# The order of TensorE products that use 128 rows and 64 rows of the array, in two stages of a two-layer encoder

## The chip, the cores and the metric

The kernel runs on one core of a Trainium2 chip. It is one launch; the metric is the device time of that launch in microseconds (us). Three runs of the kernel before are shown below, and a profile of one execution.

Five engines run side by side, each through its own list of instructions in order, and wait for each other by semaphores: TensorE (PE, matrix products into PSUM; PEld is its loading of the stationary operand), VectorE (DVE), ScalarE (ACT), GpSimd (POOL) and SyncE (SP, which here issues DMAs).

## The reference, cut to what matters

Two layers on a sequence of 1024 tokens by 1024 channels, float32. Each layer: normalise, project by a wide matrix, a mixer, gate, project back, add.

```python
def _even_mixer(...):      # layer 0: four mLSTM heads and four DeltaNet heads, each forward and backward in time
    out_a = sigmoid(mo) * head_rms(mlstm(q, k, v) + flip(mlstm(flip(q), ...)))
    out_b = head_rms(gdn(q, k, v) + flip(gdn(flip(q), ...)))
def _mlstm_chunkwise(...): # per chunk, state cmat (64 x 128 per head) and nvec
    num = w_int * einsum('bhld,bhde->bhle', qc, cmat) + einsum('bhls,bhse->bhle', sc, vc)
    den = w_int * einsum('bhld,bhd->bhl', qc, nvec) + sum(sc, -1)
def _odd_mixer(...):       # layer 1: a convolution of 31 taps and dilated attention of eight heads of 64 channels
    sc = einsum('bhrnid,bhrnjd->bhrnij', qb, kb) * dh ** -0.5 + bias    # per group of a dilation
    p = exp(sc - max(sc)); o = p @ v / sum(p)
```

## The kernel before, in words

**Products.** All products go through the helper `mm` (L119) and all transposes through `tr` (L134), so the profile shows them as L120 and L135; they are told apart by the tiles' names. Wide projections (`prod`, names `z`, `mo`, `dv`, `aq`, `ak`, `av`, `gb`, `ga`, `y`) split each float32 operand in a high and a low part and make three products of 128 rows, 128 columns and 512 elements. A product whose operands stand on 128 partitions uses all 128 rows of the array; one on 64 partitions uses a 64-row tile of it, rows 0 to 63 or 64 to 127. A plain float32 product (the mLSTM's, and the transposes) is two instructions, or passes, in the trace; those on split parts are one.

**mLSTM (layer 0, `mlstm_step`, L776).** The sequence is cut in 8 chunks of 128 tokens, and step j handles chunk j forward and chunk 7-j backward (two "direction-steps"). For each, PSUM tiles `num` (two banks, one for the even heads e=0 and one for the odd, e=1; each holds two heads q=0, 1) collect two products per head: `qt` times the state `mC` (64 rows: a head has 64 key channels) and the weights `E` times the values `mv` (128 rows, 129 elements). VectorE then makes the denominators `den`, and the output is stored; `Cps` holds the products for the next state. From step 1 on each direction-step has four products of each kind. The products of the gates' projections (`z`, `mo`) and of DeltaNet's values (`dv`) are put among them by the scheduler.

**Attention (layer 1, `attention`, L1301).** Heads are handled in four pairs `p_`, each in 8 steps i of 128 queries, so 32 steps. For each of the pair's heads e, one PSUM bank `sc` takes four products: queries `aq` times the high part of the keys `ak` (128 rows, since the low part of the queries stands in the other 64 rows) and `aq` times the low part of the keys `akl` (64 rows: 0 to 63 for e=0, 64 to 127 for e=1), each for the near group (columns c0:c1, contiguous) and for the group of dilation 4 (columns 256:512, read with a step of four elements, `r4`). The kernel issues near high, near low, dilated high, dilated low, and then the next head. VectorE adds the bias to `sc` and finds the extremes (L1336, L1338: the result is `pt`), ScalarE takes the exponentials, TensorE transposes them (`pT`, four per head), VectorE copies these to `PT` (L1363), and TensorE multiplies them by the values into `ob` (column tiles of 64). ScalarE copies `ob` to `o2`, and a DMA writes it to `od_d`. `sc` has two banks (tag "A", `BANKS` L83), one for each head.

While a pair is worked on, projections stand between its steps: `z` for the first and the third pair, `aq`, `ak`, `av` of the next pair, and, in the last pair, the first products `y` of the output.

**What sets the order.** The order on each engine isn't written by hand: a list scheduler of the framework makes it from the order of the program, the tiles' dependences and its own estimate of what is ready. An engine executes its list strictly in that order. So a change in the program's order also moves instructions that it doesn't name.

Of the kernel before, what the change touches and what calls it, by code (L numbers as in the profile page):

```python
# [17 lines left out]
P = 128  # L18
T = 1024
D = 1024  # L20
# [10 lines left out]
def t5_bucket(rel):  # L31
    # the bucket of a relative position, as the reference has it (32 buckets, 1024 at most)
    n = np.abs(rel)
    large = 8 + (np.log(np.maximum(n, 1).astype(np.float32) / np.float32(8)) / np.float32(np.log(128.0)) * np.float32(8)).astype(np.int32)
    large = np.minimum(large, 15)
    return (rel > 0).astype(np.int32) * 16 + np.where(n < 8, n, large)


def consts():
    # tables that depend on shapes alone  # L40
# [16 lines left out]
def trunk(ctx, tc, x, c, norm_g, ada_w, ada_b, ev_w_in, ev_m_gate_b, ev_dn_dt_bias, ev_dn_a_log,  # L57
# [42 lines left out]
    def behind(ins, first):  # L100
        # ins is issued after first, without a wait
# [17 lines left out]
    def mm(o, l, r, s, e):  # L119
        return nc.tensor.matmul(o, lhsT=l, rhs=r, start=s, stop=e).ins  # L120
# [16 lines left out]
    # vectors by channel  # L137
# [41 lines left out]
    def ada_sum(tiles, name):  # L179
        # sum over the chunks of d of c's SiLU times the weights; the sum over partitions is left to TensorE  # L180
# [89 lines left out]
    # gate rows: 0.. i, 32.. f, 64.. beta, 96.. decay; in each, 4 forward heads then 4 backward ones  # L270
# [86 lines left out]
    # DeltaNet keys  # L357
# [13 lines left out]
    def conv5(xp, cidx, y):  # L371
        # twice the SiLU of the convolution
# [7 lines left out]
    def conv5s(xp, cidx, y):  # L380
        # the same with ScalarE and GpSimd
# [39 lines left out]
    def modulation():  # L421
        # the rest of the modulation, a few rows of the weights with every chunk of a projection
# [79 lines left out]
    # chunk totals (rows 32.. and 96..)  # L502
# [9 lines left out]
    # running maxima of a = i - b in each chunk  # L512
# [49 lines left out]
    # the same by token: [token, chunk, 8 * quantity + dir * 4 + head]  # L562
# [24 lines left out]
    def sel_mask(ap, d):  # L587
        # keep row position l >= s (forward) or l <= s (backward); partitions are s
# [30 lines left out]
    # the lanes' results and those transposed  # L619
# [5 lines left out]
    def dn_system(ch):  # L625
# [13 lines left out]
        # the backward direction's transposed: upper triangles too  # L639
# [7 lines left out]
    def dn_inverse(n):  # L647
        # in each lane the inverse of I minus a strictly triangular 64 x 64 block, in place;
        # lanes: direction, block, chunk, head; the backward direction's blocks are transposed
# [50 lines left out]
    # gates by channel: the norm's weight, the SiLU of z and for the mLSTM half the output gate  # L700
# [56 lines left out]
    def mlstm_weights(ch):  # L757
        # weights of the pairs in the chunk, for both directions
# [18 lines left out]
    def mlstm_step(j):  # L777
        for d in range(2):
# [12 lines left out]
            pss = [bank(nm("num"), (P, 2, P + 1), "BA"[d]) for e in range(2)]  # L791
            for q in range(2):
                for e in range(2):
                    h = 2 * q + e
                    hp = slice(e * 64, e * 64 + 64)
                    if j > 0:
                        mm(pss[e][:, q, :], qt[hp, q, :], mC[d][hp, q, :], True, False)
                    pace["cps"] = mm(pss[e][:, q, :], E[:, h, :], mv[ch // 2][:, ch % 2, h, :], j == 0, True)
# [41 lines left out]
    def m_k(j):  # L840
        in0(256 + j * P, "mk", lambda hf, ps: nc.scalar.mul(out=mk[j][:, half(hf)], in_=ps, mul=0.125))
        # by token, times the weights that they enter the state with
# [44 lines left out]
    # DeltaNet over the chunks  # L887
# [4 lines left out]
    def dn_step(j):  # L892
        for d in range(2):
# [4 lines left out]
            # (I + N)^-1, transposed  # L898
# [16 lines left out]
            # decays  # L915
            # weights of the pairs in the chunk: for both directions at the first visit
# [15 lines left out]
            # v'  # L932
# [15 lines left out]
            # state  # L948
# [21 lines left out]
            # output  # L970
# [15 lines left out]
    def load_wout(w, gate, tags="h" * 16):  # L986
        # the output weights, each column times its gate
# [22 lines left out]
    def out_tile(parts, wo, use):  # L1010
        # parts [channel, token] by chunk -> psum [token, D]
# [10 lines left out]
    # scales of the summed DeltaNet outputs  # L1022
# [79 lines left out]
    # the last two by halves of the tokens: the first half's pages are free early  # L1102
# [25 lines left out]
    # the negated relative bias by relative position, one row per head  # L1128
# [13 lines left out]
    # each row again at a pitch one longer than the pitch it is read with: Toeplitz tiles  # L1142
# [46 lines left out]
    def taps(cidx):  # L1189
        # the middle one first: it reaches every token  # L1190
        for j in [15] + [j for j in range(31) if j != 15]:
            yield j - 15, cw1[:, j * 4 + cidx:j * 4 + cidx + 1]

    def conv31s(cidx, xp):
        # the same with ScalarE and GpSimd
# [65 lines left out]
    def qkv(p_):  # L1261
        # q and k as float32r parts. For each head q has its high part in the head's own rows and its low part
        # in the other rows, k has its high part in both
# [45 lines left out]
    def attention(p_, t_in):  # L1309
# [6 lines left out]
        for i in range(8):  # L1316
# [3 lines left out]
            # by group: both heads' sums, denominators and negated maxima  # L1320
            o2 = wk.tile([P, 2, 132], F32, tag="o2", name=nm("o2"))
            for e in range(2):
                hp = slice(64 * e, 64 * e + 64)
                ps = bank(nm("sc"), tag="A")
                q1, k1 = slice(i * P, i * P + P), slice(i * P - 64 + c0, i * P - 64 + c1)
                q2 = slice(hb * P, hb * P + P)
                mm(ps[:, c0:c1], Q[e][:, q1], K[e][:, k1], True, False)
                mm(ps[:, c0:c1], Q[e][hp, q1], KL[hp, k1], False, True)
                mm(ps[:, 256:512], r4(Q[e])[:, i // 2, q2], r4(K[e])[:, i // 2, :], True, False)
# [244 lines left out]
```

## Time and profile before

| | |
|---|---|
| runs | 1588.95, 1594.66, 1594.58 us; median 1594.58 |
| span of the profiled execution, first to last instruction | 1592.5 us |
| busy PE / PEld / DVE / ACT / POOL | 88% / 69% / 61% / 40% / 38% of the span |
| mean granted TensorE clock | 0.916 |
| mLSTM products `num` | 381 to 590 us of the span |
| attention scores `sc` | 1052 to 1497 us of the span |

The profile has a span and no separate time for the execution; its span lies between the runs and 2.1 us under their median. Busy shares are averages over stages with different limits, so each stage is read by itself. The granted clock is 1 at 2.4 GHz and 0.5 at 1.2 GHz. A product's record lasts longer than the time until the next one begins, because products are pipelined: what one costs the engine is the distance from its start to the next one's start.

### The profile page before, as it was taken

The page shows a single profiled execution, that of the slowest core. Times are in us where ns is not written, and L with a number is a line of the kernel's source. Part 1 is how long each engine was busy: PE and PEld are TensorE (multiplying, and loading weights), DVE is VectorE, ACT ScalarE, POOL GpSimd, SP SyncE. Part 2 cuts the span into 40 slices and gives each one's busy share as a digit, 9 for nine tenths or more (in the row PEclk, how much of TensorE's full clock was granted, in tenths as well). Part 3 has the DMA queues.
Part 4 walks back from the last instruction along what each step waited for, and adds up shares of the span by engine and source line. Part 5 has one row for each costly group of instructions (what it writes and reads, how often), then busy time and mean ns, then how long its engine had stood idle before and what let it go on. Part 6 is the DMA issues. An engine that isn't in the chain of part 4 may idle for free.

```text
span 1592.5 us, 20530 instructions
## 1 busy us (share of the span) xinstructions
PE 1407.7 (88%) x7195; PEld 1091.6 (69%) x7195; DVE 978.0 (61%) x1712; ACT 636.1 (40%) x1481; POOL 599.3 (38%) x433
## 2 busy tenths in 40 slices
PE   3978758878788999889999988689999999999998
PEld 2767646656566777778778666567776777776786
DVE  6799256999796531447745449998664433334444
ACT  5355266332444423444543233344226433324322
POOL 3452525653463521212341159986042123022210
PEclk9999878999879999889999989888899989996899
DMA  9323589345646867565552721001141142142432
GB/s 319 87 79 83 124 177 229 93 143 149 161 143 220 271 210 156 152 154 169 189 187 78 155 66 40 27 27 47 41 139 41 58 152 85 52 145 76 154 103 106
DMA packets 235659, 202.50 MB, mean 127 GB/s; under 512 B 38592, under 2 KB 198868, under 8 KB 235428
## 3 DMA queue, kind: packets, MB, share of 16 engines
q1 hardware_dynamic: 214755, 190.70, 42.1%
q10 hardware_dynamic: 20800, 10.49, 2.3%
q8 instruction: 57, 0.93, 0.2%
q14 instruction: 47, 0.38, 0.1%
HBM read 146.87 MB, written 57.93 MB: 129 GB/s over the span
## 4 chain that ended last, share of the span: by engine, by line
PE 40%; DVE 9%; DMA 4%; ACT 2%; issue 1%; POOL 0%; SPq 0%; POOLq 0%; ACTq 0%; DVEq 0%
PE y L120 9%; PE z L120 8%; DVE u L1216 7%; PE sc L120 6%; PE av L120 3%; PE ob L120 2%; PE pT L135 2%; PE aq L120 2%; PE ak L120 2%; DMA z_d<-nb_d 1%; ACT junk L1036 1%; PE gb L120 1%; PE vps L135 1%; PE T L120 1%; DMA E<-gc_d 0%
## 5 line engine op out<-in xcount | busy, mean ns | idle before, releaser
L240 POOL TENSOR_TENSOR wlo<-wraw,whi 128x1024 fp32r<-128x1024 f32 x60 | 157.2, 2621 | 239.6 <-ACT whi L239 228.2
L1216 DVE SCALAR_TENSOR_TENSOR u<-xp,cw,u 128x1009 f32<-128x1009 f32 (+14 forms) x90 | 172.8, 1920 | 2.1
L1206 POOL TENSOR_TENSOR u<-u,cv 128x512 f32<-128x512 f32 (+15 forms) x60 | 119.0, 1986 | 23.1 <-ACT cv L1205 19.8
L431 POOL TENSOR_TENSOR macc<-macc,ada 128x512 f32<-128x512 f32 x56 | 86.7, 1548 | 72.7 <-ACT ada L429 60.7
L120 PE MATMUL z<-hhi,whi 128*128 128x512 f32 x256 | 110.0, 430 | 2.3 <-DVE zt L709 2.3
L120 PE MATMUL z<-hlo,whi 128*128 128x512 f32 x256 | 109.5, 428 | 0.0
L120 PE MATMUL z<-hhi,wlo 128*128 128x512 f32 x256 | 108.4, 424 | 0.0
L239 ACT CAST whi<-wraw 128x1024 fp32r<-128x1024 f32 x60 | 62.5, 1042 | 95.2 <-PE gb L120 16.3
L120 PE MATMUL y<-wohi,mhi 128*128 128x512 f32 x240 | 96.9, 405 | 1.2 <-ACT mhi L1006 1.2
L120 PE MATMUL y<-wolo,mhi 128*128 128x512 f32 x240 | 96.1, 401 | 0.0
L120 PE MATMUL y<-wohi,mlo 128*128 128x512 f32 x240 | 95.4, 399 | 0.6 <-DVE mlo L1007 0.5
L665 DVE TENSOR_TENSOR NL<-NL,iv 128x440 f32<-128x440 f32 (+40 forms) x106 | 91.7, 894 | 0.5
L662 DVE TENSOR_TENSOR iv<-NL 128x440 f32<-128x440 f32 (+40 forms) x106 | 86.2, 845 | 1.6 <-DMA ada<-in_ada_w_dram 0.2
L1363 DVE COPY PT<-pT 128x512 f32<-128x512 f32 x48 | 32.6, 689 | 78.1 <-PE pT L135 78.0
L590 POOL TENSOR_SCALAR_AFFINE_SELECT E<-E 128x512 f32<-128x512 f32 x32 | 22.9, 715 | 147.1 <-DMA E<-nmu_d 55.3
L429 ACT ACTIVATE ada<-ada,cs 128x512 f32<-128x512 f32 x56 | 40.3, 724 | 80.6 <-DMA ada<-in_ada_w_dram 80.6
L120 PE MATMUL sc<-ak,aq 128*128 128x256 f32 (+1 forms) x128 | 61.7, 482 | 5.1 <-DVE o L1338 3.2
L120 PE MATMUL sc<-akl,aq 64*128 64x256 f32 (+1 forms) x128 | 63.6, 497 | 0.0
L120 PEld LDWEIGHTS z<-hhi,whi 128*128 128x128 f32 x256 | 52.1, 203 | 16.3 <-DVE zt L709 3.0
L1205 ACT ACTIVATE cv<-xp,cw 128x512 f32<-128x512 f32 (+15 forms) x60 | 42.2, 717 | 52.7 <-POOL u L1206 52.5
L120 PEld LDWEIGHTS z<-hlo,whi 128*128 128x128 f32 x256 | 51.9, 203 | 12.6 <-issue 1.6
L120 PEld LDWEIGHTS z<-hhi,wlo 128*128 128x128 f32 x256 | 52.0, 203 | 11.8 <-issue 0.6
(448 smaller groups left out, 3748.8 us busy)
## 6 DMA issues: line engine op xcount, KB each, us to landing
wraw<-in_ev_w_in_dram SPq DMA_DIRECT2D x32, 512.0 KB
ada<-in_ada_w_dram SPq DMA_DIRECT2D x64, 256.0 KB
wraw<-in_od_w_in_dram ACTq DMA_DIRECT2D x20, 512.0 KB
x<-in_x_dram SPq DMA_DIRECT2D x16, 512.0 KB
ada<-in_ada_w_dram SPq DMA_DIRECT2D x16, 512.0 KB
od_d<-o SPq DMA_DIRECT2D x64, 66.0 KB
n<-od_d SPq DMA_DIRECT2D x4, 1056.0 KB
E<-nmu_d SPq DMA_DIRECT2D x16, 256.0 KB
```

The source lines that it names most:

```text
L120: return nc.tensor.matmul(o, lhsT=l, rhs=r, start=s, stop=e).ins
L135: nc.tensor.transpose(o, i, ident[:k, :k])
L239: nc.scalar.copy(out=hi, in_=raw)
L240: nc.gpsimd.tensor_tensor(out=lo, in0=raw, in1=f(hi), op=ALU.subtract)
L429: nc.scalar.mul(out=t_ if k else acc, in_=t_, mul=cs[:, k:k + 1])
L431: nc.gpsimd.tensor_tensor(out=acc, in0=acc, in1=t_, op=ALU.add)
L662: nc.vector.tensor_tensor(out=t_, in0=NL[:, a_:b_, k:k + 1].to_broadcast([P, b_ - a_, m]), in1=NL[:, k:k + 1, k + 1:64].to_broadcast([P, b ...
L665: nc.vector.tensor_tensor(out=NL[:, a_:b_, k + 1:64], in0=NL[:, a_:b_, k + 1:64], in1=t_, op=ALU.add)
L1205: nc.scalar.mul(out=t_, in_=xp[:, lo + d:hi + d], mul=w_)
L1206: nc.gpsimd.tensor_tensor(out=y[:, lo:hi], in0=y[:, lo:hi], in1=t_, op=ALU.add)
L1216: nc.vector.scalar_tensor_tensor(out=y[:, lo:hi], in0=xp[:, lo + d:hi + d], scalar=w_, in1=y[:, lo:hi], op0=ALU.mult, op1=ALU.add)
L1363: nc.vector.tensor_copy(out=PT, in_=tb)
```

## The change: what it does

`mlstm_step`: the four `E`-by-`mv` products (128 rows) of a direction-step come first, one after the other, and then the four `qt`-by-`mC` products (64 rows) in the order q=1, q=0, the heads e=0 and e=1 in turn. `attention`: both heads' banks are taken together; the four 128-row products of both heads come first, then the four 64-row products. Only the first product into a bank starts an accumulation, and the last ends it, since the groups in one bank now overlap in time. The products themselves, their number and their operands stay. Comments were taken out of the file as well, and `mm` has a new argument with which the groups of one bank may overlap.

```diff
-    def mm(o, l, r, s, e):
-        return nc.tensor.matmul(o, lhsT=l, rhs=r, start=s, stop=e).ins
+    def mm(o, l, r, s, e, shared=False):
+
+        return nc.tensor.matmul(o, lhsT=l, rhs=r, start=s, stop=e, skip_group_check=shared).ins
...
             for q in range(2):
                 for e in range(2):
-                    h = 2 * q + e
-                    hp = slice(e * 64, e * 64 + 64)
-                    if j > 0:
-                        mm(pss[e][:, q, :], qt[hp, q, :], mC[d][hp, q, :], True, False)
-                    pace["cps"] = mm(pss[e][:, q, :], E[:, h, :], mv[ch // 2][:, ch % 2, h, :], j == 0, True)
+                    pace["cps"] = mm(pss[e][:, q, :], E[:, 2 * q + e, :], mv[ch // 2][:, ch % 2, 2 * q + e, :],
+                                     q == 0 or j == 0, j == 0, q > 0 and j > 0)
+            if j > 0:
+                for q in (1, 0):
+                    for e in range(2):
+                        hp = slice(e * 64, e * 64 + 64)
+                        pace["cps"] = mm(pss[e][:, q, :], qt[hp, q, :], mC[d][hp, q, :], False, q == 0, q > 0)
...
+            q1, k1 = slice(i * P, i * P + P), slice(i * P - 64 + c0, i * P - 64 + c1)
+            q2 = slice(hb * P, hb * P + P)
+            pss = [bank(nm("sc"), tag="A") for e in range(2)]
+            for e in range(2):
+                mm(pss[e][:, c0:c1], Q[e][:, q1], K[e][:, k1], True, False)
+                mm(pss[e][:, 256:512], r4(Q[e])[:, i // 2, q2], r4(K[e])[:, i // 2, :], False, False, True)
             for e in range(2):
                 hp = slice(64 * e, 64 * e + 64)
-                ps = bank(nm("sc"), tag="A")
-                q1, k1 = slice(i * P, i * P + P), slice(i * P - 64 + c0, i * P - 64 + c1)
-                q2 = slice(hb * P, hb * P + P)
-                mm(ps[:, c0:c1], Q[e][:, q1], K[e][:, k1], True, False)
-                mm(ps[:, c0:c1], Q[e][hp, q1], KL[hp, k1], False, True)
-                mm(ps[:, 256:512], r4(Q[e])[:, i // 2, q2], r4(K[e])[:, i // 2, :], True, False)
-                mm(ps[:, 256:512], r4(Q[e])[hp, i // 2, q2], r4(KL)[hp, i // 2, :], False, True)
+                mm(pss[e][:, 256:512], r4(Q[e])[hp, i // 2, q2], r4(KL)[hp, i // 2, :], False, False, True)
+                mm(pss[e][:, c0:c1], Q[e][hp, q1], KL[hp, k1], False, True)
+            for e in range(2):
+                hp = slice(64 * e, 64 * e + 64)
+                ps = pss[e]
```

TensorE's order before, one direction-step of the mLSTM (step 5; `qt` products have 64 rows, `E` products 128; the numbers tell the tiles apart, `num_3185` is the bank of the even heads and `num_3186` that of the odd):

```order
L120 MATMUL num_3185<-mC_2856,qt_3179 128x129
L120 MATMUL num_3185<-mv_1456,E_3177 128x129
L120 MATMUL num_3186<-mC_2856,qt_3179 128x129
L120 MATMUL num_3186<-mv_1456,E_3177 128x129
L120 MATMUL num_3185<-mC_2856,qt_3179 128x129
L120 MATMUL num_3185<-mv_1456,E_3177 128x129
L120 MATMUL num_3186<-mC_2856,qt_3179 128x129
L120 MATMUL num_3186<-mv_1456,E_3177 128x129
```

The same direction-step now:

```order
L121 MATMUL num_3185<-mv_1456,E_3177 128x129
L121 MATMUL num_3186<-mv_1456,E_3177 128x129
L121 MATMUL num_3185<-mv_1456,E_3177 128x129
L121 MATMUL num_3186<-mv_1456,E_3177 128x129
L121 MATMUL num_3185<-mC_2856,qt_3179 128x129
L121 MATMUL num_3186<-mC_2856,qt_3179 128x129
L121 MATMUL num_3185<-mC_2856,qt_3179 128x129
L121 MATMUL num_3186<-mC_2856,qt_3179 128x129
```

Seven changes between 64 and 128 rows inside the block have become one. Of the 56 `qt` products of the program, 54 stood alone between 128-row products before; now 12 blocks have four and one has eight.

TensorE's order before, one step of the first pair's attention (step 4; `ak` products have 128 rows, `akl` 64; `sc_8529` is e=0, `sc_8554` e=1):

```order
L135 MATMUL pT_8485<-ident,pt_8479 128x128 x4
L120 MATMUL sc_8529<-ak_8044,aq_8042 128x256
L120 MATMUL sc_8529<-akl_8046,aq_8042 128x256
L120 MATMUL sc_8529<-ak_8044,aq_8042 128x256
L120 MATMUL sc_8529<-akl_8046,aq_8042 128x256
L135 MATMUL pT_8510<-ident,pt_8504 128x128 x2
L120 MATMUL sc_8554<-ak_8045,aq_8043 128x256
L120 MATMUL sc_8554<-akl_8046,aq_8043 128x256
L120 MATMUL sc_8554<-ak_8045,aq_8043 128x256
L120 MATMUL sc_8554<-akl_8046,aq_8043 128x256
L120 MATMUL z_1433_8822<-hlo_1122_6871,whi_8817 128x512
```

The same step now (e=0 is `sc_8529`, e=1 is `sc_8530`), and behind it step 1 of the same pair:

```order
L136 MATMUL pT_8490<-ident,pt_8484 128x128 x4
L136 MATMUL pT_8510<-ident,pt_8504 128x128 x4
L121 MATMUL sc_8529<-ak_8044,aq_8042 128x256 x2
L121 MATMUL sc_8530<-ak_8045,aq_8043 128x256 x2
L121 MATMUL sc_8529<-akl_8046,aq_8042 128x256 x2
L121 MATMUL sc_8530<-akl_8046,aq_8043 128x256 x2
L121 MATMUL z_1433_8822<-hhi_1117_6866,wlo_8818 128x512
```

```order
L121 MATMUL sc_8364<-ak_8044,aq_8042 128x256
L136 MATMUL pT_8321<-ident,pt_8315 128x128 x2
L121 MATMUL sc_8364<-ak_8044,aq_8042 128x256
L121 MATMUL sc_8364<-akl_8046,aq_8042 128x256 x2
L121 MATMUL sc_8365<-ak_8045,aq_8043 128x256 x2
L121 MATMUL sc_8365<-akl_8046,aq_8043 128x256 x2
```

In the one step the order is that of the program; in the other the scheduler kept the heads apart and grouped within each head. Before, each of the 128 `akl` products stood alone; now 37 blocks have two, 8 have four, 5 have three, and 7 stand alone. In 18 of the 32 steps some product of e=1 now stands ahead of the last product of e=0; before that was so in 4 steps.

## Rows read from the trace of the kernel before

**Rows 1.** Chain of waits that ended last: shares of the span by line.
```profile
by line: PE y L120 9.3%; PE z L120 7.7%; DVE u L1216 6.6%; PE sc L120 6.1%; PE av L120 2.7%; PE ob L120 2.4%; PE pT L135 2.4%; PE aq L120 2.1%; PE ak L120 1.6%; issue 1.5%; DMA z_d<-nb_d 1.3%; ACT junk L1036 0.8%; PE gb L120 0.7%; PE vps L1
...
679.78 4.62 DMA at_d<-E
...
1452.92 2.28 DMA od_d<-o
```
**Rows 2.** Stretches: us, busy PE, PEld, DVE, ACT, POOL (instructions), clock, DMA share, GB/s.
```profile
440.00:600.00 160.00, 147.57 (x699) 108.11 (x699) 98.97 (x231) 64.53 (x137) 68.19 (x64) 0.93 0.67 212
600.00:780.00 180.00, 163.67 (x1116) 142.34 (x1115) 92.03 (x233) 76.57 (x209) 33.06 (x39) 0.92 0.63 171
...
1063.00:1200.00 137.00, 135.21 (x722) 101.10 (x723) 97.64 (x159) 48.14 (x116) 59.65 (x33) 0.89 0.22 68
1200.00:1317.00 117.00, 113.78 (x659) 85.07 (x658) 50.86 (x125) 57.43 (x129) 28.62 (x14) 0.93 0.28 92
1317.00:1426.00 109.00, 108.72 (x658) 81.64 (x657) 39.61 (x123) 35.34 (x99) 24.46 (x12) 0.97 0.24 76
1426.00:1502.00 76.00, 73.24 (x432) 52.00 (x433) 34.95 (x95) 33.00 (x90) 18.54 (x8) 0.78 0.44 138
```
**Rows 3.** Waits 592 to 780 us: who for whom, us, times, longest.
```profile
ACT E L615 <- POOL E L590: 52.8, 15, 9.4
POOL E L590 <- DMA E<-gc_d: 43.9, 10, 11.2
```
**Rows 4.** TensorE's timeline around attention: start, us, operation, rows*columns, shape, count.
```profile
1102.62 1.09 PE L135 MATMUL pT<-ident,pt 128*128 128x128 f32 x8
1103.47 0.36 PE L120 MATMUL sc<-ak,aq 128*128 128x256 f32 x1
1103.76 0.38 PE L120 MATMUL sc<-akl,aq 64*128 64x256 f32 x1
1104.07 0.60 PE L120 MATMUL sc<-ak,aq 128*128 128x256 f32 x1
1104.60 0.59 PE L120 MATMUL sc<-akl,aq 64*128 64x256 f32 x1
1105.12 0.38 PE L120 MATMUL sc<-ak,aq 128*128 128x256 f32 x1
...
1106.80 0.50 PE L120 MATMUL z<-hhi,wlo 128*128 128x512 f32 x1
```
**Rows 5.** TensorE's timeline in the mLSTM, three places.
```profile
448.44 0.68 PE L120 MATMUL num<-mv,E 128*128 128x129 f32 x4 [1.27 <-issue]
448.88 0.47 PE L120 MATMUL z<-hhi,wlo 128*128 128x512 f32 x1
...
490.05 0.72 PE L120 MATMUL S<-mq,mk 64*128 64x128 f32 x8
490.70 0.50 PE L120 MATMUL mo<-hhi,wlo 128*128 128x512 f32 x1
...
498.87 0.49 PE L120 MATMUL num<-mC,qt 64*128 64x129 f32 x2 [0.34 <-DVE E L772]
499.28 0.49 PE L120 MATMUL num<-mv,E 128*128 128x129 f32 x2
...
505.13 0.49 PE L120 MATMUL num<-mv,E 128*128 128x129 f32 x2
```
**Rows 6.** Tile sc: its products (ns min/median/max) and the first bias add.
```profile
L120 PE MATMUL sc<-akl,aq x128: 351/586/600, 1052.5 to 1497.2; 64*128 64x256 f32 x112, 64*128 64x192 f32 x16
...
L1338 DVE CUSTOM_DVE_ANT_0 pt<-sc,bias x64: 409/419/422, 1066.8 to 1499.7; 128x256 f32<-128x256 f32 x64
```
**Rows 7.** Waits 1060 to 1500 us: who for whom, us, times, longest.
```profile
DVE pt L1336 <- DMA od_d<-o: 16.4, 12, 4.1
...
PE sc L120 <- DVE o L1338: 3.2, 3, 1.5
```

## The prediction

> **What bounds the kernel now.** I read the busy table by stretch first, then the chain of waits, then TensorE's timeline inside the two stages that the change touches, and last the waits around them. In the attention stage TensorE is the bound: over the four stretches from 1063 to 1502 us it is busy 135.2 + 113.8 + 108.7 + 73.2 = 431 of 439 us [rows 2], and VectorE, the next, 223. The chain of waits says the same from the other side: the score products `sc` alone hold 6.1% of the span on it, 97 us [rows 1]. These are nearly all of them: the reader is to see that 32 steps of some 3.3 us (1103.47 to 1106.80 [rows 4]) make 107 us, less what is put between them. Whatever a step's scores cost less, the end comes earlier, as long as TensorE stays the bound.
>
> The mLSTM stage is less clear. TensorE is busy 147.6 of 160 us from 440 to 600 [rows 2], but the chain, followed back from the end, stops at 679.78 us at a DMA [rows 1] and says nothing of earlier work. Behind it, from 600 to 780 us, TensorE is busy 163.7 of 180 us, while ScalarE waits 52.8 us for GpSimd's masks and GpSimd 43.9 us for DMAs [rows 2, 3]: a stage that is part TensorE, part a sequence of other engines.
>
> **The price of a change between 64 and 128 rows.** In the mLSTM, pairs of passes of `qt` and `E` products alternate: from 498.87 to 505.13 us are 15 pairs, 0.417 us each [rows 5]. Four passes of `E` products that follow each other take 448.44 to 448.88, 0.11 us each [rows 5], so a pair without a change is 0.22. A change costs 0.417 - 0.22 = 0.197 us. The scores fit: eight transposing passes of 128 columns, with no change, take 1102.62 to 1103.47, 0.106 each; a near score product between two changes takes 1103.47 to 1103.76 and 1103.76 to 1104.07, 0.30; that is one change and 0.10 [rows 4]. A dilated one takes 0.53 (1104.07, 1104.60, 1105.12 [rows 4]), one change and 0.33.
>
> What a change costs must be partly the load of the stationary operand, which without a change goes beside the product ahead, and partly the time in which the array empties. The Trainium skill says in "TensorE: Matmul & The Clock Gate", Part 3, "The mechanism", that a load overlaps running products only when their row groups differ. By that rule grouping would leave the loads in the open; some 0.106 of each 0.197 would stay, and the gain on TensorE would be 224 × 0.09 = 20 us, for a time near 1579 with three quarters of it carried. The 0.106 and 0.11 us above, products of the same rows with a new stationary operand each, speak against it for contiguous operands; for the dilated ones no row does, and that case is kept among the rivals.
>
> **mLSTM, term by term.** Before, a direction-step has 8 pairs, 8 × 0.417 = 3.34 us. Now: eight passes of 128 rows, 8 × 0.11 = 0.88; one change, 0.20; eight passes of 64 rows on both halves of the array in turn. The last has a like in the trace: eight passes of `S`, 64 rows, heads in turn, take 490.05 to 490.70 with the change out of them, 0.65 [rows 5]. Sum 1.73, so 1.61 less. With 13 blocks in the new order that is 21 us of TensorE. Should the two halves not run side by side here, the block is 8 × 0.11 + 0.20 = 1.08, and the term 15.
>
> How much of it moves the end? If TensorE paces the stage, all; if the state's recurrence through VectorE, or the DeltaNet stage behind it, paces, nothing. I take 12, a little over half, since TensorE has 12 us idle in 160 there, and the next stage 16 in 180 [rows 2]: most of both is paced by it, but the second has waits that don't shorten [rows 3]. Bounds: 0 and 21. A side gain of no price: the `E` products no longer stand behind the `qt` ones, which need the newest state. `Cps` moves by a block and its consumer on VectorE with it; that is covered by the projections between.
>
> **Attention, term by term.** Over the whole program TensorE changes its row count 492 times before and 266 times now; at `sc` products 257 and 117 times, at `num` products 110 and 26, elsewhere 125 and 123. 140 × 0.197 = 27.6 us. This holds if a dilated product keeps its 0.33 us when it follows one of the same rows. It can be less: of these 0.33, load and stream of the moving operand, each could run beside a neighbour, and then half, 0.17, is a floor: some 121 dilated products stand in groups, 121 × 0.16 = 19 us more. And eight blocks of four have both halves of the array, 8 × 0.4 = 3 more. From below: the rule above, 140 × 0.09 = 13 us. I take 28: the change's price is what rows show, the rest isn't shown.
>
> All of the 28 should be carried: TensorE's idle time in the stage is 8 of 439 us. What is next is VectorE: per step four bias adds of 0.42 us [rows 6] and the copies of the transposes; its 223 us against TensorE's remaining 403 leave room on average. In the last pair it is tighter, as there VectorE waits for the DMA that writes `o2` away (2.28 us on the chain at 1452.92 [rows 1]; 16.4 us in 12 times in the stage [rows 7]), and 1 to 3 us of its share may stay there; I leave that within the range.
>
> The new order also holds back: both banks must be free before e=1's first product, and where that stands ahead of e=0's last, e=0's scores wait too. That can happen in the 18 steps where the order has it so. Now TensorE waits for the bias add 3.2 us in 3 times [rows 7]. I price this at nothing, since transposes and projections stand between one step's scores and the next in nearly all of them; the rival below has its price when they don't suffice.
>
> **Clock.** The granted clock is 0.89, 0.93, 0.97 and 0.78 in the four stretches [rows 2], 0.90 weighted. It is lowest in the last pair, which has the fewest projections between its steps. Shorter, denser clusters of small products should not make it worse. 0.02 of 439 us is 9 us either way; I take 0.
>
> **Sum.** 1592.5 - 28 - 12 = 1552.5 us of span, and the median of the runs lies 2.1 over the span: 1554.6.
>
> **The rivals.**
> - As forecast: both terms near the price of a change, mLSTM carried in part. 1554.6, own range 1541 to 1570. Chance 0.50.
> - More: dilated products overlap their neighbours (19 + 3), the mLSTM's 21 are carried whole, the clock gains 9: 28 + 22 + 21 + 9 = 80, so 1515; the case is everything from there to 1541. For it: TensorE's busy share in both stages. Against: all must come together. Chance 0.17.
> - Less: the loads of dilated products stay in the open, or the mLSTM's gain turns into idle time in front of the DeltaNet chain: 13 to 20 of attention and 0 of the mLSTM, 1575 to 1582. Chance 0.18.
> - No difference: the new gaps on TensorE are filled by waits for `o2`'s DMA in attention and by the recurrence in the mLSTM; 35 of 40 us given back, 1590. For it: VectorE's 12 waits [rows 7]. Against: 431 of 439. Chance 0.10.
> - Slower: the bank of e=1. In the 18 steps TensorE stands at e=1's first product until VectorE has read the step before, which itself waits for the DMA (longest 4.1 us [rows 7]). Four adds alone, 1.68 us, cost 18 × 1.68 = 30, not enough; it decides from 40 / 18 = 2.2 us. At 3 us a step, 54 - 40 gives 1609. Against: the order has transposes or projections there, and only 3.2 us of such waits now. Chance 0.05.
>
> **How the numbers follow.** About 0.5%, 8 us, is what a measurement of this kernel can tell from no change. The first three cases are faster by more: 0.85; the fourth is the same, 0.10; the fifth slower, 0.05. The range leaves out a part of the second case below and the last two above: 1522 to 1587.
>
> **What would show it.** Right: `num` blocks near 1.7 us per direction-step instead of 3.34, a step's eight scores near 2.5 us instead of 3.3, TensorE busy some 45 to 50 us less in all, and its busy share in attention still over 95%. The forecast is wrong in its sizes if near products in a group stay at 0.2 us or more, or if dilated ones fall to 0.17; wrong in its carrying if TensorE's idle time in attention rises by over 10 us, with releaser VectorE at L1338's line; wrong as a whole if `z` or `ob` products get dearer, at a lower granted clock.

## The result, and the profile after

The kernel with the new order takes 1541.48 us (median of 4 runs, 1539.62 to 1542.68) against 1593.2 us for the one before beside it: ratio 0.9676, 95% interval 0.9659 to 0.9692. The forecast was 1554.6, so the direction was right and the gain, 52 us, is 13 larger than predicted. The profiled execution has a span of 1540.9 us, 51.6 less than before.

Milestones on TensorE place these 51.6. The first score product starts at 1048.9 us (before 1052.3), the last product of `aq` and `ak` at 1446.1 (before 1496.7), and from there to the end it is 94.8 us (before 95.8). So all that lies ahead of attention gave 3.4 us, attention 47.2, the tail 1.0.

The busy table by stretch, with the columns of [rows 2], for the kernel after: first the mLSTM's stretch and the one behind it, then the four head pairs.

```profile
440.00:600.00 160.00, 133.14 (x734) 100.99 (x732) 96.44 (x228) 67.42 (x148) 71.58 (x67) 0.94 0.71 224
600.00:780.00 180.00, 161.90 (x1086) 142.33 (x1086) 94.16 (x238) 75.64 (x211) 33.51 (x38) 0.90 0.56 160
1058.00:1187.00 129.00, 122.32 (x741) 94.46 (x740) 103.25 (x165) 53.74 (x125) 64.06 (x34) 0.97 0.26 80
1187.00:1290.00 103.00, 101.44 (x650) 78.80 (x651) 52.63 (x123) 52.27 (x122) 28.31 (x13) 0.95 0.28 92
1290.00:1380.00 90.00, 89.72 (x625) 70.62 (x625) 35.28 (x116) 33.97 (x97) 22.15 (x11) 0.98 0.32 94
1380.00:1451.00 71.00, 66.99 (x437) 50.90 (x436) 39.19 (x99) 34.59 (x91) 22.09 (x9) 0.90 0.49 156
```

Two things stand in it. In the mLSTM stretch TensorE's busy time fell from 147.57 to 133.14 of the same 160 us: the work went away and idle time came in its place. In attention TensorE is still busy 380 of 393 us (before 431 of 439 [rows 2]), and its granted clock rose in all four stretches, most in the first and the last: 0.97, 0.95, 0.98, 0.90 where 0.89, 0.93, 0.97, 0.78 stood.

The chain of waits, the answer to [rows 1], shows the scores' share of the span:

```profile
by line: PE y L121 9.4%; DVE u L1220 7.8%; PE z L121 6.3%; PE sc L121 3.5%; PE av L121 2.7%; PE ob L121 2.1%; PE pT L136 2.0%; issue 1.9%; PE aq L121 1.8%; PE ak L121 1.5%; DMA z_d<-nb_d 1.3%; PE gb L121 0.7%; PE vps L136 0.7%; DMA g<-mix_d
```

`sc` is at 3.5% of 1540.9, 54 us, where it was at 6.1%, 97 us. TensorE's timeline in one step, one of the few with both heads' 64-row products in one group, shows the new order at its best; it answers to [rows 4] (start, us, operation).

```profile
1098.42 1.09 PE L136 MATMUL pT<-ident,pt 128*128 128x128 f32 x8
1099.27 1.11 PE L121 MATMUL sc<-ak,aq 128*128 128x256 f32 x4
1100.31 0.72 PE L121 MATMUL sc<-akl,aq 64*128 64x256 f32 x4
1100.96 0.50 PE L121 MATMUL z<-hhi,wlo 128*128 128x512 f32 x1
```

The eight scores take 1099.27 to 1100.96, 1.69 us, where 3.33 stood [rows 4]. The four 128-row products take 1.04 of it, the four 64-row ones 0.65. The average step is less good, as most groups hold two products: 73.2 us over 32 steps are 2.29, before 3.34. In the mLSTM (answer to [rows 5]) a direction-step reads so:

```profile
499.52 1.20 PE L121 MATMUL num<-mv,E 128*128 128x129 f32 x8 [1.24 <-ACT E L819]
500.65 0.72 PE L121 MATMUL num<-mC,qt 64*128 64x129 f32 x8
501.29 0.33 PE L136 MATMUL turn<-ident,vT 128*128 128x128 f32 x1
```

The block is 499.52 to 501.29, 1.77 us (forecast 1.73), but it stands behind 1.24 us in which TensorE waited for `E`.

All score products together, as busy time of the tile's instructions in one window (us, then PE, PEld and VectorE, clock, DMA share, GB/s), before and after:

```profile
1040.00:1500.00 460.00, 111.71 (x256) 64.91 (x256) 46.96 (x128) 0.90 0.28 86
```
```profile
1040.00:1500.00 460.00, 78.40 (x256) 52.22 (x256) 46.27 (x128) 0.96 0.31 97
```

Added up from start to next start, attention divides like this (my sums over the trace, from the first score product to the last):

| on TensorE, us | before | after | difference |
|---|---|---|---|
| scores `sc` | 107.0 | 73.2 | -34 |
| wide projections | 238.4 | 222.4 | -16 |
| transposes `pT` | 31.6 | 29.0 | -3 |
| all other products | 57.6 | 58.5 | +1 |
| idle | 11.0 | 15.2 | +4 |

The projections didn't change in number or shape over the whole program; 906 of them stand in this stretch now, 896 before. What changed is the clock: 107 of them began at the lower level before, 13 after, and their mean went from 266 to 246 ns. The granted clock stood at the lower level for 88.7 us of the stage before and for 31.8 after.

### The profile page after: what moved, and what is told of

Read it like the earlier page. It is cut to its first block, busy times and chain, and to the rows that moved or that the text cites. A ratio compares the mean times of both kernels' runs of the same rounds, so it can differ in the third digit from the quotient of the medians.

```text
span 1540.9 us, 20550 instructions
## 1 busy us (share of the span) xinstructions
PE 1338.6 (87%) x7195; PEld 1059.1 (69%) x7195; DVE 979.4 (64%) x1712; ACT 635.4 (41%) x1481; POOL 605.3 (39%) x433
## 4 chain that ended last, share of the span: by engine, by line
PE 35%; DVE 11%; DMA 4%; issue 2%; ACT 2%; POOL 0%; SPq 0%; ACTq 0%; POOLq 0%; DVEq 0%
PE y L121 9%; DVE u L1220 8%; PE z L121 6%; PE sc L121 3%; PE av L121 3%; PE ob L121 2%; PE pT L136 2%; PE aq L121 2%; PE ak L121 2%; DMA z_d<-nb_d 1%; PE gb L121 1%; PE vps L136 1%; DMA g<-mix_d 1%; ACT junk L1040 1%; PE dS L121 0%
## 5 line engine op out<-in xcount | busy, mean ns | idle before, releaser
L121 PE MATMUL z<-hhi,whi 128*128 128x512 f32 x256 | 106.8, 417 | 1.9 <-ACT mo L719 1.9
L121 PE MATMUL z<-hlo,whi 128*128 128x512 f32 x256 | 105.5, 412 | 0.0
L591 POOL TENSOR_SCALAR_AFFINE_SELECT E<-E 128x512 f32<-128x512 f32 x32 | 22.7, 709 | 149.0 <-DMA E<-gc_d 57.6
L1372 DVE COPY PT<-pT 128x512 f32<-128x512 f32 x48 | 32.4, 688 | 48.2 <-PE pT L136 48.1
L1349 ACT ACTIVATE pt<-pt,o 128x256 f32<-128x256 f32 (+1 forms) x64 | 31.4, 491 | 75.6 <-DVE o L1345 73.2
L1345 DVE CUSTOM_DVE_ANT_0 pt<-sc,bias 128x256 f32<-128x256 f32 (+1 forms) x64 | 25.8, 403 | 48.8 <-PE sc L121 28.8
```

Source lines behind the costliest of these rows:

```text
L121: return nc.tensor.matmul(o, lhsT=l, rhs=r, start=s, stop=e, skip_group_check=shared).ins
L1372: nc.vector.tensor_copy(out=PT, in_=tb)
```

## The experiments

After the result my theory was: attention gives nearly all, by the price per change and by a better clock, and the mLSTM's 22 us on TensorE come back as waits. The main rival: the mLSTM gives its 12 or more, and attention only the forecast 28.

| kernel | us, median | ratio to before, 95% | row changes at `sc` | `sc` on TensorE | lower clock in attention |
|---|---|---|---|---|---|
| before | 1593 to 1596 | 1 | 257 | 107.0 | 88.7 |
| after | 1541.48 | 0.9676 (0.9659 to 0.9692) | 117 | 73.2 | 31.8 |
| mLSTM part alone | 1590.45 | 0.9989 (0.9955 to 1.0023) | 257 | 107.4 | 81.9 |
| the same again | 1589.31 | 0.9971 (0.9939 to 1.0003) | 257 | 107.4 | 92.2 |
| attention part alone | 1549.49 | 0.9725 (0.9667 to 0.9782) | 117 | 74.1 | 48.4 |
| grouped within a head | 1557.43 | 0.9778 (0.9731 to 0.9826) | 139 | 82.8 | 47.8 |
| old order, all on 128 rows | 1525.01 | 0.9576 (0.9535 to 0.9617) | 3 | 57.7 | 27.3 |
| padded to 128 rows | 1529.56 | 0.9606 (0.9572 to 0.9640) | 3 | 56.6 | 27.3 |
| the same again | 1527.59 | 0.9558 (0.9522 to 0.9594) | 3 | 56.6 | 27.3 |
| padded, old mLSTM order | 1534.29 | 0.9612 (0.9575 to 0.9649) | 3 | 56.3 | 20.5 |
| all operands contiguous | 1527.13 | 0.9580 (0.9539 to 0.9621) | 108 | 48.1 | 34.4 |
| three `qt` buffers | 1542.30 | 0.9689 (0.9656 to 0.9721) | 117 | 73.6 | 36.7 |

The last two columns are us from the first score product to the last, my sums over each kernel's one trace. With the same 117 changes the lower level held for 31.8, 36.7 and 48.4 us, so a single trace places that time to some 15 us.

**The two parts apart.** The kernel before with the new mLSTM block alone, then with the new order of the scores alone.

```diff
+            for q in range(2):
+                for e in range(2):
+                    pace["cps"] = mm(pss[e][:, q, :], E[:, 2 * q + e, :], mv[ch // 2][:, ch % 2, 2 * q + e, :],
+                                     q == 0 or j == 0, j == 0, q > 0 and j > 0)
...
```
```diff
+            pss = [bank(nm("sc"), tag="A") for e in range(2)]
+            for e in range(2):
+                mm(pss[e][:, c0:c1], Q[e][:, q1], K[e][:, k1], True, False)
+                mm(pss[e][:, 256:512], r4(Q[e])[:, i // 2, q2], r4(K[e])[:, i // 2, :], False, False, True)
...
```

> The mLSTM block as changed, attention as before. Theory A (the 22 us that the num products save on TensorE turn mostly into idle time before and inside the DeltaNet stage, as the last num product comes 10 us earlier in the changed kernel but the first product of the output projection y only 3 us): 1587 to 1592 us against 1593 before, num about 26 us of TensorE instead of 48. Rival B (the forecast: the mLSTM term is carried by half or more, and what its trace shows is accident): 1572 to 1582.

> Attention as changed, the mLSTM block as before. Theory A (attention brought 47 us: 34 by the scores and 13 by the higher granted clock of the products beside them): 1543 to 1549 us, scores 73 us instead of 107, lower-clock time between the first and the last score near 35 us instead of 89. Rival B (attention brought the 28 to 31 us of the forecast, the clock's part depends on the mLSTM's timing by chance): 1560 to 1567.

Measured: 0.9989 and 0.9725. The attention part alone makes most of the gain, 0.0275 of 0.0324; the mLSTM part's interval reaches 1. In the run of the mLSTM part alone the stretch from 1055 to 1490 us keeps a clock of 0.91, as before (0.90), so the better clock comes with the new order of the scores and not with the mLSTM's. The attention part alone ended at the upper edge of what was expected, with 48.4 us at the lower level where 35 was.

**Grouped within a head.** Is it the number of changes that counts, or that both heads' halves of the array stand side by side? Here the four products of a head are grouped as high, high, low, low, one bank after the other.

```diff
 for e in range(2):
     mm(ps[:, c0:c1], Q[e][:, q1], K[e][:, k1], True, False)
+    mm(ps[:, 256:512], r4(Q[e])[:, i // 2, q2], r4(K[e])[:, i // 2, :], False, False, True)
+    mm(ps[:, 256:512], r4(Q[e])[hp, i // 2, q2], r4(KL)[hp, i // 2, :], False, False, True)
     mm(ps[:, c0:c1], Q[e][hp, q1], KL[hp, k1], False, True)
-    mm(ps[:, 256:512], r4(Q[e])[:, i // 2, q2], r4(K[e])[:, i // 2, :], True, False)
-    mm(ps[:, 256:512], r4(Q[e])[hp, i // 2, q2], r4(KL)[hp, i // 2, :], False, True)
```

> Attention only: each head's four products grouped (two of 128 rows, then two of 64), one head after the other with its own bank as before; 139 changes of row count at sc products instead of 257 (117 in the changed kernel). Theory A (the number of changes pays): 118 of 140 changes saved, so 35 to 42 us less than before, 1551 to 1558. Rival C (most comes from both heads together: the two 64-row halves of the array side by side and both banks taken at once): 15 us less at most, 1578 or more.

Measured: 1557.43 us, scores 82.8 us with 139 changes. Both count. The 118 changes that went, at 0.197 each, make 23 of the 24 us by which the scores fell. The kernel after, with 22 changes fewer, should then have 78.5; it has 73.2 (74.1 in the attention part alone). The 4 to 5 us between are what the halves side by side bring; only 13 of the after kernel's 57 groups of 64-row products hold more than two. The groups themselves show it: at the higher clock four products on the two halves in turn take 0.65 us on average (7 groups), and two on one half 0.64 (33 groups), so the other half's pair takes next to no time of its own.

**The same old order without any change of rows.** The strictest test of the price is the order of before, attention and mLSTM, with the low products on all 128 rows. They then also sum over the other head's channels, so the scores are not the reference's.

```diff
-                mm(ps[:, c0:c1], Q[e][hp, q1], KL[hp, k1], False, True)
+                mm(ps[:, c0:c1], Q[e][:, q1], KL[:, k1], False, True)
-                mm(ps[:, 256:512], r4(Q[e])[hp, i // 2, q2], r4(KL)[hp, i // 2, :], False, True)
+                mm(ps[:, 256:512], r4(Q[e])[:, i // 2, q2], r4(KL)[:, i // 2, :], False, True)
```

> The order of before in both stages, but the akl products take all 128 partitions (so the correction by the low part of the keys also sums over the other head's channels; the outputs differ from the reference): no change of row count between score products, 3 instead of 257. Theory A (the change is what costs, not the order): a step's eight products fall to 1.5 to 1.7 us, sc 50 to 55 us in all, 1533 to 1545. Rival C (the order and the banks matter): 1580 or more. If a load can't run beside products of the same rows, the spacing of near products stays near 0.2 us and the time near 1570.

Measured: 1525.01 us, scores 57.7 (50 to 55 expected), 225 ns each. With 254 changes fewer and nothing regrouped the scores lost 49.3 us, 0.194 per change, near the 0.197 of the prediction, read from 15 pairs in another stage. A part of it is the clock: counted from the scores that begin at the higher level alone, and scaled to all 256, they fell from 103.3 us to 56.7, 0.183 per change; by the kernel grouped within a head, at 81.2, it is 0.187. So it is the change, not the order as such. The end came 68 us earlier where 48 to 60 were expected, because the wide projections beside the scores fell too, from 238.4 to 217.7 us.

All products have the same rows here, and a record of a weight load lasts 186 ns at least, yet near products follow each other every 0.14 us (timeline of the next kernel): the load is hidden. The records show when it starts. These are the loads of a near low product, in the kernel before (behind a change) and in the next kernel (no change):

```profile
1103.76 0.18 PEld L120 LDWEIGHTS sc<-akl,aq 64*128 64x128 f32 x1
```
```profile
1091.48 0.21 PEld L121 LDWEIGHTS sc<-akl,aq 128*128 128x128 f32 x1
```

The first starts together with its own product (1103.76 [rows 4]), the second with the product ahead, 0.14 us before its own (1091.62). Over all scores at the higher clock the load leads by 0.002 us behind a change and by 0.12 without one (medians, before and next kernel). The Trainium skill ("TensorE: Matmul & The Clock Gate", Part 3, "The mechanism") lists a load as overlapping running products only when their row groups differ; this trace does not agree. The same section also lets a load go ahead when it goes to a background weight buffer, which would fit; no run here shows where a load goes.

**Padded to 128 rows.** If that is so, a kernel with the whole computation and hardly a change should beat the new order. Attention goes back to its old order, head by head, and the low keys stand in one tile per head, with zeros in the other head's 64 rows.

```diff
-        KL, vT_ = page(nm("akl"), dt=F32R, tag="h"), page(nm("av"))
+        KL, vT_ = [page(nm("akl"), dt=F32R, tag="h") for e in range(2)], page(nm("av"))
+        for e in range(2):
+            nc.gpsimd.memset(f(KL[e][64 - 64 * e:128 - 64 * e]), 0.0)
...
+                mm(ps[:, c0:c1], Q[e][:, q1], KL[e][:, k1], False, True)
+                mm(ps[:, 256:512], r4(Q[e])[:, i // 2, q2], r4(KL[e])[:, i // 2, :], False, True)
```

> mLSTM as changed; attention in the old order, with the low part of the keys in two tiles of 128 partitions, the other head's rows filled with zeros by GpSimd, so all score products have 128 rows and the result is the full one. Theory A (the change of rows is the price): no change of row count between score products (3 instead of 117), sc about 58 us as with the unpadded 128-row products, 1520 to 1530, some 15 us under the changed kernel. Rival D (the 8 further fills on GpSimd and two more large tiles hold back the queries' and keys' projections, where GpSimd's splits of the weights pace TensorE): 1535 or more.

Measured: 1529.56 us, and 1527.59 in a second set of runs: 12 to 14 us under the kernel after (by the ratios 11 to 19), the fastest here that leaves the computation whole. Twice the rows per low product cost less than the change to half the rows. It isn't the zeros that make them cheap: the kernel without zeros has 57.7 us of scores, this one 56.6. TensorE's timeline of that kernel (columns as above):

```profile
1090.94 0.49 PE L121 MATMUL sc<-ak,aq 128*128 128x256 f32 x1
1091.25 0.42 PE L121 MATMUL sc<-akl,aq 128*128 128x256 f32 x1
1091.48 0.30 PE L121 MATMUL sc<-ak,aq 128*128 128x256 f32 x1
1091.62 0.29 PE L121 MATMUL sc<-akl,aq 128*128 128x256 f32 x1
1091.75 0.48 PE L121 MATMUL sc<-ak,aq 128*128 128x256 f32 x1
1092.05 0.41 PE L121 MATMUL sc<-akl,aq 128*128 128x256 f32 x1
1092.28 0.41 PE L121 MATMUL z<-hhi,whi 128*128 128x512 f32 x1
```

A near product costs 0.14 and 0.13 us, a dilated one 0.30 and 0.23; before they were 0.30 and 0.53 [rows 4]. The differences, 0.16 to 0.30, lie about the price of a change. What is left to gain shows too: TensorE is idle 26.8 us in attention, against 15.2 in the kernel after.

**All operands contiguous.** The dilated products cost twice the near ones also without a change. This is the kernel after, with these reading 128 and 256 neighbouring tokens in place of every fourth; their scores are of other tokens.

```diff
+            c4 = slice(i // 2 * 256, i // 2 * 256 + 256)
...
-                mm(pss[e][:, 256:512], r4(Q[e])[:, i // 2, q2], r4(K[e])[:, i // 2, :], False, False, True)
+                mm(pss[e][:, 256:512], Q[e][:, q1], K[e][:, c4], False, False, True)
-                mm(pss[e][:, 256:512], r4(Q[e])[hp, i // 2, q2], r4(KL)[hp, i // 2, :], False, False, True)
+                mm(pss[e][:, 256:512], Q[e][hp, q1], KL[hp, c4], False, False, True)
```

> The changed kernel, with the dilated group's operands read as contiguous columns (so these scores are of other tokens; the outputs differ from the reference): prices the step of four elements. Theory A (a dilated operand takes about twice the time to load and to stream, and within a group this can't be hidden, since its neighbours are shorter): a step's eight products 1.0 to 1.2 us instead of 1.7, sc 45 to 55 us, 1515 to 1527. Rival E (within a group loads and streams of dilated products already run beside each other, as the forecast's larger case had it): within 5 us of the changed kernel.

Measured: 1527.13 us, scores 48.1 us in place of 73.2; about 14 of these 25 us reach the end. Most of the 25 is the step of four elements. Groups of like make show its price at the higher clock: two 64-row products of one head fell from 0.64 to 0.43 us, four 128-row ones from 1.04 to 0.64, so 0.20 to 0.22 per dilated product. The rest is order: 9 changes of rows went as well, 2 us, and 14 groups of four 64-row products stand where 8 stood. The tile's rows show where the step acts: durations of the weight loads and products (ns min/median/max), after and then contiguous.

```profile
L121 PEld LDWEIGHTS sc<-ak,aq x128: 186/307/339, 1048.7 to 1445.9; 128*128 128x128 f32 x128
L121 PE MATMUL sc<-ak,aq x128: 250/440/577, 1048.9 to 1446.1; 128*128 128x256 f32 x112, 128*128 128x192 f32 x16
```
```profile
L121 PEld LDWEIGHTS sc<-ak,aq x128: 186/190/338, 1044.7 to 1422.6; 128*128 128x128 f32 x128
L121 PE MATMUL sc<-ak,aq x128: 248/298/580, 1045.0 to 1422.7; 128*128 128x256 f32 x112, 128*128 128x192 f32 x16
```

The median load falls from 307 to 190 ns: with a step of four a load is slower by 0.12 us, and the product too.

**Where the mLSTM's gain goes.** Its products fell from 50.27 to 28.23 us of busy time, 22.0, as forecast (21); the tile's rows from 440 to 600 us, before and after:

```profile
440.00:600.00 160.00, 50.27 (x232) 35.18 (x232) 16.91 (x92) 8.98 (x32) 0.93 0.67 212
```
```profile
440.00:600.00 160.00, 28.23 (x232) 23.69 (x232) 15.02 (x92) 9.12 (x32) 0.94 0.71 224
```

TensorE's waits from 440 to 590 us (who for whom, us, times, longest), before:

```profile
PE mo L120 <- DVE zt L709: 5.5, 2, 5.3
PE Cps L120 <- DVE mC L830: 3.6, 1, 3.6
PE num L120 <- DVE E L772: 1.8, 2, 1.4
```

and after:

```profile
PE Cps L121 <- DVE mC L834: 6.4, 1, 6.4
PE num L121 <- DMA E<-es_d: 4.7, 3, 1.8
PE mo L121 <- DVE zt L710: 3.6, 1, 3.6
PE num L121 <- DVE E L773: 3.0, 2, 1.6
PE num L121 <- POOL qt L790: 2.9, 4, 1.5
PE num L121 <- ACT E L819: 2.2, 3, 1.2
```

The makers of `E`, `qt` and `mC` are now late: 12.4 us of idle time from 440 us to the last `num` product became 26.4. If `qt` were the one that paces, a third buffer for it should bring the stage forward. The kernel after with that alone:

```diff
-                qt = pm.tile([P, 2, P], F32, tag="qt", name=nm("qt"), bufs=2)
+                qt = pm.tile([P, 2, P], F32, tag="qt", name=nm("qt"), bufs=3)
```

> The changed kernel with three qt buffers instead of two. Theory F (the mLSTM's num products now wait for qt and E, which DMAs bring through two buffers, and that is where half of its gain stays): TensorE's idle time from 440 us to the last num product falls from 26 to 20 us or less, that product comes 4 to 7 us earlier, and the end 2 to 7 us. Rival G (the state's recurrence and E hold it): no difference beyond 2 us at either.

Measured: 1542.30 us, ratio 0.9689 (0.9656 to 0.9721): no difference to the kernel after. The last `num` product came 5.5 us earlier (574.0 for 579.5), as expected, but not because TensorE waited less: its idle time up to there is 25.9 us from 440 us on, where it was 26.4 and 20 or less was expected. The new list has 398 wide products between the first and the last `num`, where the kernel after has 411, which take 106.7 us there in place of 112.7; the other 13 stand behind it now. The first product of the DeltaNet stage (`T`) stayed at 588.7 (589.1). So a third `qt` buffer feeds nothing faster, and which of the makers holds the mLSTM is not shown.

The mLSTM part alone was run again, since its interval reached 1; its kernel is the one above.

> The mLSTM block alone once more, since its first interval (7 us faster to 4 slower) leaves open whether it brings anything. Theory A' (its last product comes 10 us earlier in both traces; what is left of that at the end hangs on the granted clock in the DeltaNet stage, which had from 17 to 38 us of the lower level in traces of equal order there): 1582 to 1589, a ratio of 0.993 to 0.998. Rival B' (nothing is carried): 1590 to 1596, ratio 0.998 to 1.002.

Measured: 0.9971, again with 1 inside the interval. Last, the same part where attention has hardly a change left: the padded kernel with the old mLSTM order, and the padded kernel again beside it.

```diff
+                    if j > 0:
+                        mm(pss[e][:, q, :], qt[hp, q, :], mC[d][hp, q, :], True, False)
+                    pace["cps"] = mm(pss[e][:, q, :], E[:, h, :], mv[ch // 2][:, ch % 2, h, :], j == 0, True)
...
```

> The padded attention as in the experiment before, 1529.6 us with the mLSTM block in its new order; here that block stands in its old order, pair by pair. So the difference to the next run is the mLSTM part alone, measured where attention has hardly a row change left. Theory P (the 21 us of TensorE turn into waits for E, qt and mC, and into a DeltaNet stage that begins little earlier): 2 to 6 us, as the two runs of the mLSTM part alone gave, 1532 to 1535. Rival F (the forecast, TensorE paces over half of that stage): 12 us, 1542. Rival N (the part moves nothing): 1530. Num products 48 us on TensorE in each case, last num near 590 us.

> The same kernel as the padded one before, with the mLSTM in its new order, beside the run with the old order on one chip: 1527 to 1533. Theory P wants it 2 to 6 us under that run, rival F 12 us, rival N no difference.

Measured: 0.9612 with the old order; 0.9558 and 0.9606 with the new. That is 9 us by one comparison and 1 us by the other, so this pair does not separate the forecast's 12 from 4 on its own. With the two runs of the part alone (2 and 5 us) and after against attention alone (0.0049, 8 us), each weighted by its interval, it comes to about 4 us, 1 to 7. Twelve is outside.

The traces of all these kernels show where the rest stays. In the five kernels with the old order the last `num` product starts at 590.5 us on average (589.0 to 592.9) and the first `y`, behind the DeltaNet stage, at 785.6; in the six with the new order and two `qt` buffers at 579.5 (576.7 to 582.9) and 780.0. So of 22 us on TensorE half are lost inside the mLSTM, where its idle time from the first to the last `num` rose from 23.2 to 35.4 us on average. Of the 11 that are left about 5.5 are lost in the DeltaNet stage: it takes 190.7 us from its first product to `y` where it took 186.3, and starts 1 us later behind the last `num`. There ScalarE and GpSimd wait as they did [rows 3] (us, times, longest; kernel after):

```profile
POOL E L591 <- DMA E<-gc_d: 50.6, 9, 10.3
ACT E L616 <- POOL E L591: 42.4, 12, 6.4
```

Together 93.0 us of waits, where 96.7 stood: the mLSTM's earlier end did not shorten them. Two things go with the 4.4 us by which the stage itself is longer. Nine wide products that stood in the mLSTM stand in it now (225 for 216, some 1.5 us of its time). And its length goes with the granted clock: in the new order it took 186.4 and 188.5 us in the two traces with 17 us at the lower level, and 192.3 to 194.7 in the three with 34 to 38; the old order had 17 to 27 us. Why the clock stood lower there stays open.

## Why the prediction was right in direction and 13 us short

- **The price of a change, 0.197 us: right within a tenth.** Three kernels with 257, 139 and 3 changes have 107.0, 82.8 and 57.7 us of scores: 0.205 and 0.194 per change, of which the clock makes a part; at the higher clock alone it is 0.187 and 0.183. The load that no longer runs ahead is in the records; how much of the price is the emptying of the array, which the prediction also names, no run shows.
- **Attention's term, 28: too small by 6.** At the higher clock alone the scores fell from 103.3 to 72.3 us, 31. The changes are 140 × 0.185 = 26 of it, and the two halves of the array side by side about 5 (forecast 3, and left out of the 28). The other 3 of the 34 came because the lower clock touched fewer scores. The further 19 for dilated products were a bound that was not reached in the new order: they fell only to 0.27 in the padded kernel, from the 0.33 assumed.
- **Carried whole: right.** TensorE stayed the bound of the stage, at 97% busy. Its idle time rose by 4 us, under the 10 that were named as the sign of a wrong carrying. VectorE's waits for `o2`'s DMA are 18.3 us (before 16.4 [rows 7]), and the bank of e=1, the slower rival, cost little. The waits after (us, times, longest):

```profile
PE sc L121 <- DVE o L1347: 3.8, 2, 2.0
DVE pt L1345 <- DMA od_d<-o: 18.3, 9, 4.9
```

  TensorE waited for the bias add 3.8 us in 2 times where it waited 3.2 in 3 [rows 7]: of that rival's 54 us, 0.6 show.
- **Clock, 0 ± 9: the step that failed most.** It gave 16 us in the wide projections of attention alone. The forecast had the row with the most room, 0.78 in the pair with the fewest projections [rows 2], and said only that denser clusters should not make it worse. The time at the lower level falls with the changes: 82 to 92 us with 257, 47.8 with 139, 32 to 48 with 117, 20 to 27 with 3. That this is cause and not company is not shown apart: no run changed the clock alone. TensorE's busy time fell by 69 us in all (1407.7 to 1338.6), where the prediction named 45 to 50 as the sign of being right.
- **mLSTM: 21 saved was right (22.0), 12 carried was wrong.** It carried about 4. The step that failed is "TensorE has 12 us idle in 160 there", read as TensorE pacing most of the stage. A nearly full engine can have a second chain close behind it: the waits for `E`, `qt` and `mC` after the change show one in the mLSTM, and [rows 3] shows one behind it.

So the sum that the runs show is 34 + 16 + 3 - 1 - 4 = 48 in attention and about 4 from the mLSTM, 52, in place of 28 + 12. The errors had opposite signs, 20 too little and 8 too much, so that the forecast missed by only 13 is in part luck. The result stands at the edge between the forecast's own range and the rival "more" (1541), by half of that rival's reasons: the clock and the halves, not the mLSTM.

## What to carry to other kernels

Where products of 64 and 128 rows alternate, count the changes and price each at what one pair with and one without it show in the trace; then ask first whether the half-height operand can be padded with zeros to full height, which here beat both groupings that were tried. Ask of each saved microsecond whether the next engine's chain stands close behind: a stretch with 8% idle time on one engine says little about what paces it, and the products' waits after a smaller change would have said it. Look at the granted clock on both sides too: here it gave 16 us in products that the change doesn't name, against a forecast of 28 for all of attention. It went with the number of changes, though no run shows what moved it.

## What the runs showed of the hardware

- A 128-row product of 128 columns and 256 elements with a new stationary operand follows a like one every 0.13 to 0.14 us; with a change of rows ahead of each it was 0.30.
- The stationary operand read with a step of four elements loads in 0.31 us and not 0.19, and a product with both operands so costs 0.23 to 0.30 us and not 0.13.
- A change between 64 and 128 rows costs 0.18 to 0.20 us in three stretches of work: the mLSTM's pairs, the scores grouped within a head, and the scores all on 128 rows.
- Four 64-row products on the two halves in turn, two near and two dilated, take 0.65 us with their change, and two on one half 0.64 with theirs; four on 128 rows take 1.04 with theirs. Less a change each, two halves in turn cost about half of the same products on all rows.
